# GpSimd leaves the chunk's tail and the S5 gate, the memory's norm takes other PSUM banks, and the final norm's factor is read from PSUM

## The chip, the cores and the metric

The kernel runs on one core of a Trainium2 chip. The metric is the device time of one execution, in microseconds (us): the median of several runs. A profiled execution of the same program gives the trace from which all durations below are taken. The engines are TensorE (PE, matmuls and transposes by matmul), VectorE (DVE), ScalarE (ACT), GpSimd (POOL) and SyncE (SP), which here issues all the DMAs.

## The reference

One decoder layer in float32 with 1024 tokens and width 1024. Its parts, cut to what matters here:

```python
def _mixer(xn, ...):
    proj = xn @ w_in                          # q, k, v, z, a, b and the S5 input u
    qkv = silu(_causal_dwconv(proj[..., OFF_Q:OFF_Z], conv_w))     # width 4, per channel
    g = -exp(dn_a_log) * softplus(a + dn_dt_bias); beta = sigmoid(b)
    o = _gated_delta_rule(l2norm(q) * dk**-0.5, l2norm(k), v, g, beta)
    o = o * rsqrt(mean(o * o, -1) + EPS)
    o = o * dn_norm_g * silu(z)               # 4 heads of 128
    y = gelu(_s5(u, ...))
    y = y * sigmoid(y @ s5_w_glu + s5_b_glu)  # the S5 gate, width 512
    return concatenate([o, y], -1) @ w_out

h = h + _mixer(_rmsnorm(h), ...)
h = h + _cross_attn(_rmsnorm(h), mem, ...)    # 256 memory tokens, themselves normalised:
                                              # mn = _rmsnorm(mem, norm_mem_g)
h = h + (silu(hn @ w_gate) * (hn @ w_up)) @ w_down
return _rmsnorm(h, norm_final_g)              # the final norm
```

## The kernel before, in words

Features lie on partitions (128 at a time) and tokens along the free dimension, in halves of 512. Each float32 operand of a large matmul is split into a high part (ACT, line 62) and the rest (line 63, on DVE or POOL), and each product is three matmuls (lines 79 to 81).

The kernel is written with a tile framework. Every tile comes from a pool with a fixed number of buffers; a tile that finds none free waits until an older one of its name has been read for the last time. The order of the instructions on each engine's queue is not the order of the text: the framework simulates a timeline at build time (`schedule_with_timeline_sim=True`), places each instruction where it becomes ready there, and takes the earlier one in the text where two are ready. The queues then run strictly in that order. `issue_after` and `keep_in_program_order` fix the order in a few places, none of which the diff touches.

PSUM has eight banks of 128 x 512 float32. The pool `pm` (name "mm") has three for the large products throughout. `p5` (name "aux") has one until the mixer ends. `px`, `pda`, `pdb`, `p6`, `ps`, `po` and, for the second half of the kernel, `pa` (five banks, name "aux") share the rest in turn.

The stages in the order of the text, with the functions that the change and the prediction's steps name:

1. `x_prep`, `in_tile` for the four S5 inputs, `s5_setup` and `s5_pre` (parameters of the S5 model; the product of line 334 uses p5), `zab` (z, a, b; z goes to DRAM as zD).
2. `gates` computes g and beta on small tiles (L545 writes g). Two products with a triangular matrix follow: L552 (copied by L554, its exponential by L556) and L558, whose copy `gr` (L560) goes to DRAM as gD. Each head later reads a row of gD back, spread over all partitions, as `d_Qg`.
3. `mem_prep` loads the memory, squares it, sums the squares over features (`rstd`, L120 to L129), spreads the factor over the partitions by four matmuls into a bank `rb` (L821), and multiplies the memory by it and by the gain (L826, eight instructions on DVE). The results are split on ACT and POOL and stay until `mem_proj` uses them.
4. For each of four heads: `in_tile` for k, q and v. A half tile is 24 matmuls into a bank of pm; L480 multiplies it by the norm's factor into `pre`; L489 (ACT) and three L491 (DVE) build the convolution in a bank of p5; L492 (ACT, silu) writes `it`. `dn_a` transposes k (L595), takes d_Qg through POOL (L583) and ACT (L584 to L586), copies two columns on DVE (L588, L589) and prepares the head's matrices; `dn_b` inverts them.
5. Eight chunks of 128 tokens. `dn_seq` carries the state of all four heads from chunk to chunk (L752, L754, L760, L761 on ACT, L766, L769) and leaves the chunk's output in a bank `po`. `dn_tail` normalises it, multiplies it by silu(z) and transposes it: squares on ACT (L791), L792, ten small rsqrt steps on DVE (L85 to L89), the product with the factor (L795, DVE), the product with z (L796, POOL), four transposes (L799), a split (L65, L66). Beside it run the memory's projections (`mem_proj`) and the S5 blocks (`s5_in`, `s5_out`).
6. `glu`, the S5 gate: for two halves and four row tiles, twelve matmuls into a bank of p5 or p6, a sigmoid on ACT (L909) into an SBUF tile, y from its two parts on DVE (L910), the product on POOL (L911), a split.
7. `out_acts`, `out_pair` (out projection), `mem_load` (whose tiles `kst` take buffers that the chunk stage frees), cross attention, then the feed-forward stage as Strassen products.
8. The last rows: for three pieces of 512, 256 and 256 tokens, `ff_down` and the residual add (L1368), squares and their sum, and `final`: the norm's factor spread by matmuls (`row_sums`, L143), copied to SBUF by ACT (`rowbc`, L139), then for eight row tiles a multiply on DVE (even ones, with the gain, L1380) or POOL (odd ones, L1378; their gain was applied before), and a store for every two.

Of the kernel before, what the change touches and what calls it, by code (L numbers as in the profile page):

```python
# [9 lines left out]
F32 = mybir.dt.float32  # L10
F32R = mybir.dt.float32r
I32 = mybir.dt.int32
AF = mybir.ActivationFunctionType
ALU = mybir.AluOpType
# [4 lines left out]
P = 128  # L19
NT = 1024  # L20
HT = 512
# [24 lines left out]
class Kernel:  # L46
# [478 lines left out]
    def gates(self, ab, cv):  # L525

        v, A = self.v, self.a
        ts, st, tt = v.tensor_scalar, v.scalar_tensor_tensor, v.tensor_tensor
        T = lambda n: cv.tile([P, 8, 4], F32, name=n, bufs=1)
        x, e, u, l, d, m = (T("gt_" + n) for n in "xeuldm")  # L530
        tt(out=x, in0=ab[:, :, 0:4], in1=self.dtb.unsqueeze(1).to_broadcast([P, 8, 4]), op=ALU.add)

        st(out=l, in0=x, scalar=-1.0, in1=x, op0=ALU.mult, op1=ALU.min)
        self.exact_exp(e, l, u, d, m)
        ts(out=u, in0=e, scalar1=1.0, scalar2=2.0, op0=ALU.mult, op1=ALU.add)
        v.reciprocal(out=u, in_=u)
        tt(out=u, in0=u, in1=e, op=ALU.mult)
        tt(out=d, in0=u, in1=u, op=ALU.mult)
        ts(out=l, in0=d, scalar1=2.0 / 17, scalar2=0.0, op0=ALU.mult, op1=ALU.add)
        for k in range(15, 1, -2):  # L540
            st(out=l, in0=l, scalar=2.0 / k, in1=d, op0=ALU.add, op1=ALU.mult)
        st(out=l, in0=l, scalar=2.0, in1=u, op0=ALU.add, op1=ALU.mult)
        st(out=l, in0=x, scalar=0.0, in1=l, op0=ALU.max, op1=ALU.add)
        g_ = T("gt_g")
        tt(out=g_, in0=l, in1=self.nega.unsqueeze(1).to_broadcast([P, 8, 4]), op=ALU.mult)  # L545
        beta = self.cp.tile([P, 8, 4], F32, name="beta")
        ts(out=x, in0=ab[:, :, 4:8], scalar1=-1.0, scalar2=0.0, op0=ALU.mult, op1=ALU.add)
        self.exact_exp(e, x, u, d, m)
        ts(out=e, in0=e, scalar1=1.0, scalar2=1.0, op0=ALU.add, op1=ALU.mult)
        v.reciprocal(out=beta, in_=e)  # L550
        ps = self.p5.tile([P, HT], F32, name="aux")
        self.te.matmul(ps[:, 0:32], self.UT, g_.rearrange("p a b -> p (a b)"), start=True, stop=True)  # L552
        gc = self.cp.tile([P, 8, 4], F32, name="gc")
        v.tensor_copy(out=gc, in_=ps[:, 0:32].rearrange("p (a b) -> p a b", a=8))  # L554
        eg = self.cp.tile([P, 8, 4], F32, name="eg")
        A.activation(out=eg, in_=gc, func=AF.Exp)  # L556
        ps = self.p5.tile([P, HT], F32, name="aux")
        self.te.matmul(ps[0:32, 0:P], g_.rearrange("p a b -> p (a b)"), self.UT, start=True, stop=True)  # L558
        gr = cv.tile([32, P], F32, name="gr", bufs=1)
        v.tensor_copy(out=gr, in_=ps[0:32, 0:P])  # L560
        self.load(self.gD, gr)
        self.gate = (beta, gc, eg)
        self.dnv = [self.cp.tile([P, 8, 4], F32, name="dn_" + n) for n in ("al", "b3n", "eq")]
# [216 lines left out]
    def dn_tail(self, c, po, dq, xs):  # L780

        v, A, g, te = self.v, self.a, self.g, self.te
        sh = [P, 4, P]
        eq = self.dnv[2][:, c, :]
        T = lambda name: self.slot(name).rearrange("p (h v) -> p h v", h=4)
        sz = T("sz")
        self.load(sz, self.zD[c].rearrange("p (h v) -> p h v", h=4))
        on = T("on")
        sso, ro, w4 = (dq.tile([P, 4], F32, name="d_" + n) for n in ("sso", "ro", "w4b"))
        for i in range(4):  # L790
            A.activation(out=on[:, i], in_=po[:, i], func=AF.Square, accum_out=sso[:, i:i + 1])  # L791
        v.scalar_tensor_tensor(out=sso, in0=sso, scalar=1.0 / P, in1=eq, op0=ALU.mult, op1=ALU.add)  # L792
        self.rsqrt(ro, sso, w4)
        on = T("on")
        v.tensor_tensor(out=on, in0=po, in1=ro.unsqueeze(2).to_broadcast(sh), op=ALU.mult)  # L795
        g.tensor_tensor(out=on, in0=on, in1=sz, op=ALU.mult)  # L796
        ps = self.po.tile(sh, F32, name="po")
        for i in range(4):
            te.transpose(ps[:, i], on[:, i], self.ident)  # L799
        o = slice((c % 4) * P, (c % 4 + 1) * P)  # L800
        self.split(ps, *(x[:, 0:4, o] for x in xs[c // 4]), self.dng)


    def mem_prep(self, cv):

        T = lambda n, i: self.tmp.tile([P, HT], F32, name=n, bufs=i)
        two = lambda t: t.rearrange("p (k t) -> p k t", k=2)
        raws = [T(n, 2) for n in ("res", "res", "fsg")] + [cv.tile([P, 4 + HT], F32, name="pre", bufs=3)[:, 4:]]
        acc = T("acc0", 1)
        for i, r in enumerate(raws):  # L810
            self.load(two(r), self.I["memT"][:, 2 * i:2 * i + 2])
            sq = T("sq", 2) if i else acc
            self.a.activation(out=sq, in_=r, func=AF.Square)
            if i:
                self.g.tensor_tensor(out=acc, in0=acc, in1=sq, op=ALU.add)
        self.g.tensor_tensor(out=acc[:, 0:NMEM], in0=acc[:, 0:NMEM], in1=acc[:, NMEM:], op=ALU.add)
        ps = lambda: self.p5.tile([P, HT], F32, name="aux")
        rs = self.rstd(acc, 2, "rsm", ps())
        rb = ps()
        for t in range(2):  # L820
            self.te.matmul(rb[:, t * P:(t + 1) * P], rs[:, t:t + 1].to_broadcast([P, P]), self.ident, start=True, stop=True)  # L821
        mh, ml = [], []
        for i, ns in enumerate((("fsg", "sq"), ("sq", "acc1"), ("acc0", "res"), ("res", "fsg"))):
            for j in range(2):
                r = two(raws[i])[:, j]
                self.v.scalar_tensor_tensor(out=r, in0=r, scalar=self.gain(2, 2 * i + j), in1=rb[:, 0:NMEM], op0=ALU.mult, op1=ALU.mult)  # L826
            h, l = (T(n, 1 if n[0] == "a" else 2).bitcast(F32R) for n in ns)
            self.split(raws[i], h, l, None, self.g)
            mh += [two(h)[:, j] for j in range(2)]
            ml += [two(l)[:, j] for j in range(2)]  # L830
        return mh, ml
# [58 lines left out]
    def glu(self, q8, xs):  # L890
        T = lambda n, k=2: q8.tile([P, HT], F32, name=n, bufs=k)
        ws = []
        for m in range(4):
            raw = q8.tile([P, 4, P], F32, name="yr", bufs=2)
            self.load(raw, self.I["w_glu"][m])
            wh, wl = (q8.tile([P, 4, P], F32R, name=n, bufs=4) for n in ("gwh", "gwl"))
            self.split(raw, wh, wl, None, self.g)
            ws.append((wh, wl))
        y8 = [[x[:, 4:8] for x in xs[h]] for h in range(2)]
        for h in range(2):  # L900
            yh, yl = y8[h]
            out = []
            for m in range(4):
                wh, wl = ws[m]
                ps = (self.p5, self.p6)[m % 2].tile([P, HT], F32, name="aux")
                for k in range(4):
                    self.mm3(ps, wh[:, k], wl[:, k], yh[:, k], yl[:, k], k == 0, k == 3)
                sg, yy = T("yr"), T("yy", 8)
                self.a.activation(out=sg, in_=ps, func=AF.Sigmoid, bias=self.bglu[:, m:m + 1])  # L909
                self.v.tensor_tensor(out=yy, in0=yh[:, m].bitcast(F32), in1=yl[:, m].bitcast(F32), op=ALU.add)  # L910
                self.g.tensor_tensor(out=yy, in0=yy, in1=sg, op=ALU.mult)  # L911
                out.append(yy)
            for m in range(4):
                self.split(out[m], yh[:, m], yl[:, m])
# [455 lines left out]
    def final(self, o, rs):  # L1370

        n = o.stop - o.start
        rb = self.tmp.tile([P, HT], F32, name="res", bufs=2)[:, 0:n]
        self.rowbc(rs, n // P, rb)
        for m in range(KD):
            dst = self.out_rows(m, o)
            if m % 2 == 1:
                self.g.tensor_tensor(out=dst, in0=dst, in1=rb, op=ALU.mult)  # L1378
            else:
                self.v.scalar_tensor_tensor(out=dst, in0=dst, scalar=self.gain(4, m), in1=rb, op0=ALU.mult, op1=ALU.mult)  # L1380
            if m % 2:
                h = o.start // HT
                src = self.hT[:, m // 2, 2 * h:2 * h + 2, o.start - h * HT:o.stop - h * HT]
                self.load(self.out[m - 1:m + 1].rearrange("m p t -> p m t")[:, :, o], src)
# [295 lines left out]
```

## Time and profile before

| | |
|---|---|
| median of 3 runs | 1603.62 us (1600.15 to 1607.66) |
| the profiled execution | 1605.2 us |
| its span in the trace | 1603.2 us |
| instructions | 20926 |
| mean granted clock of TensorE | 0.958 |

The trace's views used below are: the page (busy time and share of each engine, the chain that ended last), busy time by stretches, the waits (who waited for whom: total, times, longest), groups of instructions (either busy time and mean, or the shortest, median and longest duration), and the timeline (start, duration, engine, line, operation, output and inputs, how many, and in brackets how long the engine had been idle before and what ended that). All times are in us from the span's start, unless marked ns. A line number is that of the kernel before. L85 to L89 and other helpers serve several places; the tile's name tells which. In the names, `d_R` and `d_L` are also reused as spare buffers in the chunk stage: there L795 and L796 write `on` into d_R and read z from d_L. An "aux" tile may be in p5, p6 or pa.

### The profile page before, as it was taken

The page shows a single profiled execution, that of the slowest core. Times are in us where ns is not written, and L with a number is a line of the kernel's source. Part 1 is how long each engine was busy: PE and PEld are TensorE (multiplying, and loading weights), DVE is VectorE, ACT ScalarE, POOL GpSimd, SP SyncE. Part 2 cuts the span into 40 slices and gives each one's busy share as a digit, 9 for nine tenths or more (in the row PEclk, how much of TensorE's full clock was granted, in tenths as well). Part 3 has the DMA queues.
Part 4 walks back from the last instruction along what each step waited for, and adds up shares of the span by engine and source line. Part 5 has one row for each costly group of instructions (what it writes and reads, how often), then busy time and mean ns, then how long its engine had stood idle before and what let it go on. Part 6 is the DMA issues. An engine that isn't in the chain of part 4 may idle for free.

```text
span 1603.2 us, 20926 instructions
## 1 busy us (share of the span) xinstructions
PE 1457.7 (91%) x7326; PEld 1218.8 (76%) x7326; DVE 1188.9 (74%) x2164; ACT 634.7 (40%) x1137; POOL 655.9 (41%) x475
## 2 busy tenths in 40 slices
PE   6887699996978788999999999999999998999985
PEld 4787488886877576878888788888888886777864
DVE  8969489886699797775546697666666668899886
ACT  5222353452544563454443442333333334533322
POOL 6175234324552416620010443333333347766544
PEclk9999899997989988999999999999999999999997
DMA  7256454548688152245524414444444357444302
GB/s 224 80 164 199 134 133 124 140 119 293 213 291 265 47 197 105 79 131 171 171 92 165 144 33 145 149 142 139 145 137 137 112 168 251 149 146 150 126 10 105
DMA packets 146616, 237.49 MB, mean 148 GB/s; under 512 B 12464, under 2 KB 79440, under 8 KB 143952
## 3 DMA queue, kind: packets, MB, share of 16 engines
q1 hardware_dynamic: 146512, 236.17, 45.7%
q8 instruction: 57, 0.93, 0.2%
q14 instruction: 47, 0.39, 0.1%
HBM read 169.69 MB, written 68.53 MB: 149 GB/s over the span
## 4 chain that ended last, share of the span: by engine, by line
PE 53%; DVE 24%; DMA 9%; issue 5%; ACT 4%; POOL 3%; SPq 1%; DVEq 0%; POOLq 0%; ACTq 0%
PE aux L81 9%; PE aux L79 9%; PE aux L80 9%; PE mm L81 8%; PE mm L79 8%; PE mm L80 8%; DVE aux L491 2%; DVE wlo L63 1%; DVE d_R L675 1%; DMA s_wb<-in_s5bT 1%; DVE s_S L398 1%; POOL wlo L63 1%; DVE hT L1380 1%; DMA d_R<-LD 1%; DMA wraw<-in_w_xk 1%
## 5 line engine op out<-in xcount | busy, mean ns | idle before, releaser
L62 ACT ACTIVATE whi<-wraw 128x1024 fp32r<-128x1024 f32 (+2 forms) x152 | 139.7, 922 | 202.3 <-PE mm L80 67.3
L79 PE MATMUL mm<-AH,whi 128*128 128x512 f32 x448 | 178.4, 399 | 1.4 <-DVE hT L1325 1.4
L81 PE MATMUL mm<-AH,wlo 128*128 128x512 f32 x432 | 170.9, 396 | 0.0
L80 PE MATMUL mm<-AL,whi 128*128 128x512 f32 x408 | 161.3, 396 | 0.0
L150 POOL TENSOR_TENSOR acc<-acc,sq 128x512 f32<-128x512 f32 (+1 forms) x41 | 53.1, 1295 | 212.9 <-ACT sq L149 212.1
L63 DVE TENSOR_TENSOR wlo<-wraw,whi 128x1024 fp32r<-128x1024 f32 (+1 forms) x76 | 97.9, 1290 | 33.2 <-ACT whi L62 33.1
L1204 POOL TENSOR_TENSOR sg<-sg,ca 128x512 f32<-128x512 f32 x40 | 58.2, 1456 | 144.1 <-DVE sg L1197 92.7
L63 POOL TENSOR_TENSOR wlo<-wraw,whi 128x1024 fp32r<-128x1024 f32 x28 | 67.8, 2422 | 115.8 <-ACT whi L62 98.8
L79 PEld LDWEIGHTS mm<-AH,whi 128*128 128x128 f32 x448 | 84.6, 189 | 20.9 <-DVE hT L1325 2.9
L81 PEld LDWEIGHTS mm<-AH,wlo 128*128 128x128 f32 x432 | 81.5, 189 | 18.3 <-issue 0.4
L80 PEld LDWEIGHTS mm<-AL,whi 128*128 128x128 f32 x408 | 77.1, 189 | 16.6
L80 PE MATMUL aux<-AL,whi 128*128 128x512 f32 x216 | 85.0, 393 | 0.7 <-POOL AL L63 0.7
L79 PE MATMUL aux<-AH,whi 128*128 128x512 f32 x176 | 69.7, 396 | 0.0
L62 ACT ACTIVATE wlo<-graw 128x512 fp32r<-128x512 f32 x62 | 38.8, 626 | 62.7 <-PE aux L81 53.1
L81 PE MATMUL aux<-AH,wlo 128*128 128x512 f32 x160 | 63.4, 396 | 0.0
L491 DVE SCALAR_TENSOR_TENSOR aux<-pre,convw,aux 128x512 f32<-128x512 f32 x72 | 54.1, 751 | 8.3 <-ACT aux L489 7.5
L1202 ACT ACTIVATE ca<-ca 128x512 f32<-128x512 f32 x40 | 25.3, 633 | 83.5 <-DVE ca L1197 83.0
L63 POOL TENSOR_TENSOR wlo<-wb,whi 128x768 fp32r<-128x768 f32 x19 | 39.8, 2094 | 42.3 <-ACT whi L62 42.3
L81 PE MATMUL aux<-AH,whi 128*128 128x512 f32 x136 | 53.4, 392 | 0.0
L80 PEld LDWEIGHTS aux<-AL,whi 128*128 128x128 f32 x216 | 40.6, 188 | 10.6 <-POOL AL L63 1.4
L63 DVE TENSOR_TENSOR wlo<-graw,wlo 128x512 fp32r<-128x512 f32 x40 | 46.0, 1150 | 2.2 <-ACT wlo L62 2.2
L79 PE MATMUL aux<-AH,wlo 128*128 128x512 f32 x120 | 47.3, 394 | 0.0
(713 smaller groups left out, 4678.2 us busy)
## 6 DMA issues: line engine op xcount, KB each, us to landing
graw<-in_w_up SPq DMA_DIRECT2D x22, 512.0 KB
acc<-in_w_down SPq DMA_DIRECT2D x42, 256.0 KB
actD<-sg SPq DMA_DIRECT2D x40, 256.0 KB
WD<-acc SPq DMA_DIRECT2D x40, 256.0 KB
wraw<-in_w_in SPq DMA_DIRECT2D x16, 512.0 KB
d_X<-XD SPq DMA_DIRECT2D x8, 1024.0 KB
wraw<-AD SPq DMA_DIRECT2D x16, 512.0 KB
wraw<-VD SPq DMA_DIRECT2D x16, 512.0 KB
```

The source lines that it names most:

```text
L62: self.a.activation(out=hi, in_=src, func=AF.Copy)
L63: return (eng or self.v).tensor_tensor(out=lo, in0=src, in1=hi.bitcast(F32), op=ALU.subtract)
L79: mm(ps, wh, xh, start=first, stop=False)
L80: mm(ps, wh, xl, start=False, stop=False)
L81: mm(ps, wl, xh, start=False, stop=last)
L150: eng.tensor_tensor(out=acc, in0=acc, in1=tmp, op=ALU.add)
L398: v.tensor_tensor_scan(out=Zs[:, k, q], data0=self.m8[:, 2 * b + q:2 * b + q + 1].to_broadcast([P, P]), data1=Z[:, k, q], initial=0.0, op0 ...
L491: v.scalar_tensor_tensor(out=acc, in0=pre[:, 1 + i:1 + i + HT], scalar=cw(i), in1=acc, op0=ALU.mult, op1=ALU.add)
L675: tt(out=R[:, i, :, 0:i], in0=R[:, i, :, 0:i], in1=X[:, :, 0:i], op=ALU.mult)
L1202: A.activation(out=r, in_=r, func=AF.Silu)
L1204: g.tensor_tensor(out=r, in0=r, in1=sg[o], op=ALU.mult)
L1380: self.v.scalar_tensor_tensor(out=dst, in0=dst, scalar=self.gain(4, m), in1=rb, op0=ALU.mult, op1=ALU.mult)
```

## The change

- `gates` and `mem_prep`: the tiles for the gates' two products, for the memory's sum of squares and for its spread factor come from pm instead of p5.
- `dn_tail`: DVE multiplies the chunk's output by z instead of by the rsqrt factor; then ACT multiplies each of the four heads by its factor, as a per-partition scale. POOL's product is gone.
- `glu`: the sigmoid is written back into its own PSUM bank, and DVE multiplies from there. POOL's product and the SBUF tile for the sigmoid are gone.
- `final`: the DVE multiplies read the factor from its PSUM bank, and row tile 7 moves from POOL to DVE. POOL still reads ACT's copy in SBUF.

```diff
--- before.py
+++ after.py
@@ -548,13 +548,13 @@
         self.exact_exp(e, x, u, d, m)
         ts(out=e, in0=e, scalar1=1.0, scalar2=1.0, op0=ALU.add, op1=ALU.mult)
         v.reciprocal(out=beta, in_=e)
-        ps = self.p5.tile([P, HT], F32, name="aux")
+        ps = self.pm.tile([P, HT], F32, name="mm")
         self.te.matmul(ps[:, 0:32], self.UT, g_.rearrange("p a b -> p (a b)"), start=True, stop=True)
         gc = self.cp.tile([P, 8, 4], F32, name="gc")
         v.tensor_copy(out=gc, in_=ps[:, 0:32].rearrange("p (a b) -> p a b", a=8))
         eg = self.cp.tile([P, 8, 4], F32, name="eg")
         A.activation(out=eg, in_=gc, func=AF.Exp)
-        ps = self.p5.tile([P, HT], F32, name="aux")
+        ps = self.pm.tile([P, HT], F32, name="mm")
         self.te.matmul(ps[0:32, 0:P], g_.rearrange("p a b -> p (a b)"), self.UT, start=True, stop=True)
         gr = cv.tile([32, P], F32, name="gr", bufs=1)
         v.tensor_copy(out=gr, in_=ps[0:32, 0:P])
@@ -792,8 +792,9 @@
         v.scalar_tensor_tensor(out=sso, in0=sso, scalar=1.0 / P, in1=eq, op0=ALU.mult, op1=ALU.add)
         self.rsqrt(ro, sso, w4)
         on = T("on")
-        v.tensor_tensor(out=on, in0=po, in1=ro.unsqueeze(2).to_broadcast(sh), op=ALU.mult)
-        g.tensor_tensor(out=on, in0=on, in1=sz, op=ALU.mult)
+        v.tensor_tensor(out=on, in0=po, in1=sz, op=ALU.mult)
+        for i in range(4):
+            A.activation(out=on[:, i], in_=on[:, i], func=AF.Copy, scale=ro[:, i:i + 1])
         ps = self.po.tile(sh, F32, name="po")
         for i in range(4):
             te.transpose(ps[:, i], on[:, i], self.ident)
@@ -814,7 +815,7 @@
             if i:
                 self.g.tensor_tensor(out=acc, in0=acc, in1=sq, op=ALU.add)
         self.g.tensor_tensor(out=acc[:, 0:NMEM], in0=acc[:, 0:NMEM], in1=acc[:, NMEM:], op=ALU.add)
-        ps = lambda: self.p5.tile([P, HT], F32, name="aux")
+        ps = lambda: self.pm.tile([P, HT], F32, name="mm")
         rs = self.rstd(acc, 2, "rsm", ps())
         rb = ps()
         for t in range(2):
@@ -905,10 +906,10 @@
                 ps = (self.p5, self.p6)[m % 2].tile([P, HT], F32, name="aux")
                 for k in range(4):
                     self.mm3(ps, wh[:, k], wl[:, k], yh[:, k], yl[:, k], k == 0, k == 3)
-                sg, yy = T("yr"), T("yy", 8)
-                self.a.activation(out=sg, in_=ps, func=AF.Sigmoid, bias=self.bglu[:, m:m + 1])
+                yy = T("yy", 8)
+                self.a.activation(out=ps, in_=ps, func=AF.Sigmoid, bias=self.bglu[:, m:m + 1])
                 self.v.tensor_tensor(out=yy, in0=yh[:, m].bitcast(F32), in1=yl[:, m].bitcast(F32), op=ALU.add)
-                self.g.tensor_tensor(out=yy, in0=yy, in1=sg, op=ALU.mult)
+                self.v.tensor_tensor(out=yy, in0=yy, in1=ps, op=ALU.mult)
                 out.append(yy)
             for m in range(4):
                 self.split(out[m], yh[:, m], yl[:, m])
@@ -1370,14 +1371,18 @@
     def final(self, o, rs):
 
         n = o.stop - o.start
+        ps = self.pa.tile([P, HT], F32, name="aux")
+        self.row_sums(rs, n // P, ps)
         rb = self.tmp.tile([P, HT], F32, name="res", bufs=2)[:, 0:n]
-        self.rowbc(rs, n // P, rb)
+        self.a.activation(out=rb, in_=ps[:, 0:n], func=AF.Copy)
         for m in range(KD):
             dst = self.out_rows(m, o)
-            if m % 2 == 1:
+            if m in (1, 3, 5):
                 self.g.tensor_tensor(out=dst, in0=dst, in1=rb, op=ALU.mult)
+            elif m == 7:
+                self.v.tensor_tensor(out=dst, in0=dst, in1=ps[:, 0:n], op=ALU.mult)
             else:
-                self.v.scalar_tensor_tensor(out=dst, in0=dst, scalar=self.gain(4, m), in1=rb, op0=ALU.mult, op1=ALU.mult)
+                self.v.scalar_tensor_tensor(out=dst, in0=dst, scalar=self.gain(4, m), in1=ps[:, 0:n], op0=ALU.mult, op1=ALU.mult)
             if m % 2:
                 h = o.start // HT
                 src = self.hT[:, m // 2, 2 * h:2 * h + 2, o.start - h * HT:o.stop - h * HT]
```

## The prediction

> **What bounds the kernel now.** I read the page first, then busy time by stretches, then the waits and the timeline of the stretches where TensorE (PE) is not full.
>
> ```profile
> PE 1457.7 (91%) x7326; PEld 1218.8 (76%) x7326; DVE 1188.9 (74%) x2164; ACT 634.7 (40%) x1137; POOL 655.9 (41%) x475
> 700.00:1300.00 600.00, 596.74 (x2638) 486.55 (x2639) 380.93 (x595) 221.38 (x384) 159.11 (x112) 1.00 0.40 133
> 168.50:188.80 20.30, 12.82 (x60) 10.28 (x58) 1.79 (x12) 3.17 (x4) 6.31 (x3) 0.91 0.62 182
> 181.30:196.00 14.70, 0.04 (x2) 0.03 (x1) 7.11 (x16) 8.09 (x11) 9.21 (x6) 0.63 0.21 65
> 196.00:270.00 74.00, 72.29 (x368) 60.67 (x368) 64.45 (x150) 31.49 (x68) 27.57 (x13) 0.98 0.44 122
> 440.00:506.00 66.00, 53.34 (x403) 51.88 (x404) 59.48 (x144) 29.54 (x73) 27.74 (x27) 0.90 0.81 269
> 506.00:545.00 39.00, 35.11 (x217) 30.17 (x216) 31.78 (x76) 22.83 (x54) 17.85 (x13) 1.00 0.45 147
> 545.00:556.00 11.00, 4.58 (x21) 3.27 (x19) 6.68 (x16) 4.83 (x15) 4.58 (x3) 0.90 0.00 0
> 1560.00:1603.20 43.20, 23.06 (x136) 22.04 (x136) 24.72 (x57) 11.13 (x28) 20.58 (x23) 0.71 0.28 97
> ```
>
> Behind each stretch stand its length, then the busy time (and instructions) of PE, weight loads, VectorE (DVE), ScalarE (ACT) and GpSimd (POOL), then PE's granted clock. From 700 to 1300 PE is full, and the change touches nothing there. It touches three places where PE is not full: a hole at 181 to 196, the chunk stage from 440 to 556, where DVE is the fullest engine, and the end. So the sum is made from these three.
>
> **The hole: the gates and the memory's norm.** The waits there, and the timeline around it:
>
> ```profile
> PE da L595 <- ACT it L492: 14.7, 1, 14.7
> 150.92 0.19 DVE L545 TENSOR_TENSOR gt_g<-gt_l,nega 128x32 f32<-128x32 f32 x1
> 160.43 0.30 PE L552 MATMUL aux<-gt_g,cst 128*128 128x32 f32 x2
> 160.50 0.67 DVE L480 TENSOR_TENSOR pre<-mm,rbx 128x512 f32<-128x512 f32 x1
> 168.22 0.27 DVE L560 COPY gr<-aux 32x128 f32<-32x128 f32 x1
> 168.65 0.23 PE mm L79
> 175.14 0.62 SPq L54 DMA_DIRECT2D gD<-gr  x1
> 186.62 2.36 POOL L63 TENSOR_TENSOR wlo<-wraw,whi 128x1024 fp32r<-128x1024 f32 x1
> 188.79 0.22 DVE L588 COPY dn_al<-d_Qg 128x8 f32<-128x8 f32 x1 [13.67 <-ACT d_Qg L586]
> 191.27 0.86 DVE L826 SCALAR_TENSOR_TENSOR pre<-pre,gains,aux 128x256 f32<-128x256 f32 x2
> 192.23 0.69 ACT L489 ACTIVATE aux<-pre,convw 128x512 f32<-128x512 f32 x1 [0.21 <-DVE pre L826]
> 192.97 2.32 DVE L491 SCALAR_TENSOR_TENSOR aux<-pre,convw,aux 128x512 f32<-128x512 f32 x3
> ```
>
> The first convolution's input is ready at 161.2 (L480), yet its first step, L489, starts at 192.23, right behind the last L826. L826 applies the memory's norm. The norm's factor lies in the single p5 bank, which the convolution's accumulator needs too. L826 in turn stands on DVE behind L588, which waits for the gate's round trip through DRAM (gr, gD, d_Qg). So PE's transposes (L595) of the finished tile come 14.7 us late.
>
> After: the factor lies in pm, p5 is free at 161, and no convolution needs L826. From 168.5 to 188.8 DVE was busy 1.8 of 20.3 us. The work that now may go there is five convolutions (5 x 2.3), three L480 (3 x 0.7) and L826 (188.9 to 192.1, 3.2): 16.8 us, and it fits. What is late next is a weight: its low part (POOL, 186.62) stands behind the same round trip and ends at 189.0, and PE would reach it at 181.3 + 24 x 0.23 + 0.6 for the transposes = 187.4, so 1.6 us of wait come back.
>
> The norm's factor now holds one of pm's three banks until L826 is done; a bank is a half tile, 24 x 0.23 = 5.5 us of PE. The gates' two products (L552, L558) go from p5 to pm as well: g was ready at 151.1 and its product ran at 160.4, when p5 came free. With it the copy gr and the DMAs gD and d_Qg move forward on SP's queue, past the loads that held gD from 168.5 to 175.1; that shortens L588's wait and takes from nothing but those loads. If the order stays, it brings nothing.
>
> Bounds: 14.7, plus 1.1 for the slow matmuls that follow a hole (clock 0.63), is the most; nothing if L491 stays behind L588; a loss of 5.5 if only pm's bank counts. PE is full from 196 to 270 (72.29 of 74), so what it wins there it keeps. 14.7 + 1.1 - 1.6 = 14.2, less 2.2 (my estimate, two thirds of L826) for norm steps that still come first on DVE: **12 us gained** (-5.5 to 16).
>
> **The chunk's tail and the S5 gate.** Timeline, groups of lines (busy, mean ns) and waits:
>
> ```profile
> L87 DVE TENSOR_TENSOR d_w4b<-d_ro 128x4 f32<-128x4 f32 x24 | 9.0, 374 | 0.6
> L89 DVE SCALAR_TENSOR_TENSOR d_ro<-d_w4b,d_ro 128x4 f32<-128x4 f32 x24 | 6.4, 268 | 0.6
> L88 DVE SCALAR_TENSOR_TENSOR d_w4b<-d_w4b,d_sso 128x4 f32<-128x4 f32 x24 | 6.0, 248 | 0.6
> 546.48 0.16 DVE L792 SCALAR_TENSOR_TENSOR d_sso<-d_sso,dn_eq 128x4 f32<-128x4 f32 x1 [5.66 <-ACT d_R L791]
> 547.10 1.30 POOL L911 TENSOR_TENSOR yy<-yy,yr 128x512 f32<-128x512 f32 x1 [3.53 <-ACT yr L909]
> 547.28 1.14 DVE L89 SCALAR_TENSOR_TENSOR d_ro<-d_w4b,d_ro 128x4 f32<-128x4 f32 x1
> 552.97 1.59 POOL L796 TENSOR_TENSOR d_R<-d_R,d_L 128x512 f32<-128x512 f32 x1 [1.95 <-issue]
> 554.62 1.11 PE L799 MATMUL po<-cst,d_R 128*128 128x128 f32 x4 [6.15 <-POOL d_R L796]
> 555.86 1.74 SPq L54 DMA_DIRECT2D kst<-memD  x4
> L791 ACT ACTIVATE d_R<-po x32: 269/278/300, 439.6 to 546.1; 128x128 f32<-128x128 f32 x32
> POOL d_R L796 <- issue: 11.2, 3, 7.6
> POOL d_R L796 <- DVE d_R L795: 8.3, 4, 2.4
> ```
>
> A DVE step of 0.16 us takes 1.14 beside a POOL multiply; both read two operands from SBUF. The 72 rsqrt steps took 9.0 + 6.4 + 6.0 = 21.4 instead of 72 x 0.16 = 11.5, so 9.9 us were lost beside POOL work of every kind. The 16 multiplies that go are 37% of POOL's 43 instructions here, so 3.7 of these.
>
> The last chunk's tail is on the path: the next stage's loads (kst, 555.86) need its buffers, 9.4 us after L792. After the change: L792 and ten rsqrt steps at 0.2 from start to start (546.48 to 547.28 is four), 2.2; two gate products and two splits on DVE between them at 0.68, 2.7; four scaled copies on ACT at 0.28, 1.1; one ACT step between, 0.7; the last transpose, 0.5. That is 7.2: 2.2 gained. Of the 3.7, 2.0 lie in that tail, and of the other 1.7 I count half, 0.8, since waits cover the rest. The tail's product stays on DVE, with another operand.
>
> Edits at no cost, and their cover: six of the eight new gate products on DVE (8 x 0.68 = 5.4) lie under PE's gate matmuls, the last two are counted above; 28 of the 32 scaled copies (8 x 1.1 = 8.8) lie in ACT's idle time, 36 of 66 us. With the cover gone they cost 14.2. Waits that are added: p5 and p6 come free after the DVE product and not after the sigmoid, 0.7 us later, while the next tile's 12 matmuls (2.8) run in the other bank; the z tile is now waited for on DVE, the rsqrt steps behind it, but two slots let its load go out two chunks ahead. The most is 9.4 - 3.8 (rsqrt, copies and transpose alone) + 1.7 = 7.3. **3 us gained** (-14 to 7).
>
> **The final norm.** Timeline, two lines' durations, and one piece of the chain:
>
> ```profile
> 1572.08 6.92 DVE L1380 SCALAR_TENSOR_TENSOR hT<-hT,gains,res 128x512 f32<-128x512 f32 x4 [1.88 <-ACT res L139]
> 1572.12 6.33 POOL L1378 TENSOR_TENSOR hT<-hT,res 128x512 f32<-128x512 f32 x4 [2.33 <-PE aux L81]
> 1579.47 0.66 PE L120 MATMUL aux<-ones,acc 128*128 128x64 f32 x2 [4.47 <-DVE hT L1368]
> 1588.90 3.64 DVE L1380 SCALAR_TENSOR_TENSOR hT<-hT,gains,res 128x256 f32<-128x256 f32 x4 [1.22 <-ACT res L139]
> 1596.35 3.31 POOL L1378 TENSOR_TENSOR hT<-hT,res 128x256 f32<-128x256 f32 x4 [4.09 <-ACT res L139]
> L1325 DVE TENSOR_TENSOR Q<-Q,aux x48: 672/675/689, 1384.5 to 1545.6; 128x512 f32<-128x512 f32 x48
> 207.18 1.23 DVE d_kd L600
> ```
>
> Four 512-wide DVE steps take 6.92 here beside POOL's four. With one operand in PSUM a DVE step stays at 0.672 to 0.689 (L1325, 48 times, POOL busy beside many). So five steps make 3.4 in the first piece: 3.5 gained, and PE waited 4.47 for their end. In the second, five of half the width at 0.36 make 1.8: 1.8 gained. The third ends on POOL, whose three steps without a two-operand DVE step beside them I put at 0.73 each, an estimate from L911's 1.30 for twice the width plus a little: 2.2 for 3.3, 1.1 gained. The bank is now held until the last DVE step, which keeps PE from one 256-wide tile, 0.7. The stores follow their pairs. 3.5 + 1.8 + 1.1 - 0.7 = 5.7: **6 us gained** (2 to 8).
>
> I do not count the time of ACT's copy: L600 started at 207.18, when ACT was done with the same bank, though it needs no result of ACT, so DVE will wait for the copy as before. The Trainium skill, "PSUM — Partial Sum Buffer", section "PSUM bank collisions raise a hardware error", has the same: two engines' accesses to one bank are put in order, reads too. Against the change speaks the Trainium skill, "VectorE: DVE Perf Modes", section "The TRN2 errata": a VectorE step has 120 fixed cycles from PSUM and 58 from SBUF. By that, an estimate of 0.065 us more for each of 23 steps, the gain would be 1.5 us less; the trace does not agree, L1325 reads PSUM at 0.675.
>
> **Sum.** The profiled execution took 1605.2 with its span of 1603.2, 1.6 above the median of 1603.62. 1605.2 - 12 - 3 - 6 = 1584.2; I say 1584. The runs of one kernel lie up to 0.5% (8 us) apart, which is the bound of "same" below.
>
> **The rivals.** First, the hole stays. The order of each queue comes from a timeline that the framework simulates at build time, and it may still put L588 ahead of the convolutions; it did put it ahead of L826. Against it: L480 was ready 27 us before L588. Then 1605.2 - 3 - 6 = 1596.2.
>
> Second, slower: ACT inherits POOL's wait. POOL waited 19.5 us (11.2 + 8.3) before L796, at no one's cost. If the scaled copies stand on ACT ahead of the state chain's own copy (L761) while rsqrt is late on a crowded DVE, every chunk waits. 19.5 + 8.8 = 28.3 lost in place of the 3 gained: 1605.2 - 12 - 6 + 28.3 = 1615.5. It decides from 18 us, 2.6 in each of seven chunks. Against it: with fewer POOL multiplies rsqrt is less late.
>
> Third, the new order makes waits of its own in places that the change doesn't name and eats about half: 1595 (1588 to 1602).
>
> **How the numbers follow.** All three gains, 0.54, its own range 1574 (16 + 7 + 8) to 1592 (8 + 1 + 4). The hole stays, 0.20, and the new order, 0.15, each about half below 1595.6, which is 8 under the median. Slower, 0.11. Faster 0.54 + 0.10 + 0.07 = 0.71, same 0.18, slower 0.11. The range from 1573 to 1601 leaves out the slower case and the far end of the third.
>
> **What would show it.** L489's first start near 161 to 170, and no idle time over 5 us before the first L595; no POOL rows at L796 or in the gate; about 7 us from the last L792 to the kst loads; the final norm's DVE steps at 0.68 and 0.42. I am wrong if L588 still stands before the convolutions, if ACT idles before the scaled copies with L761 behind them, or if PE waits for a pm bank between 100 and 190.

## The result, and the profile after

The changed kernel takes 1590.44 us (median of 4 runs, 1587.80 to 1592.99) against 1605.64 of the kernel before (4 runs, three of them those of the table above). These medians lie 15.2 us apart; the ratio on record is 0.9872, 95% interval 0.9840 to 0.9904, which is some 20 us. Measured again beside 17 runs of the kernel before it was 0.9874 (0.9857 to 0.9891; 1589.6 against 1610.37), and there medians and ratio agree on 20 us. So it is 15 to 21 us faster, and 20 by the measurement with more runs. The prediction said 1584 and faster; the time is 6 us above it and inside the range. The parts did not bring what it gave them, as the experiments show.

The profiled execution took 1592.23 us, its span 1590.2. First the busy time by stretches. Columns: length, then busy time (and instructions) of PE, weight loads, DVE, ACT and POOL, then PE's granted clock. Before:

```profile
0.00:160.00 160.00, 126.63 (x713) 106.41 (x714) 132.54 (x386) 54.15 (x84) 83.51 (x95) 0.91 0.53 166
160.00:200.00 40.00, 24.79 (x109) 19.78 (x108) 18.07 (x45) 11.89 (x16) 11.61 (x7) 0.83 0.46 137
200.00:260.00 60.00, 60.00 (x305) 50.34 (x304) 50.80 (x122) 29.22 (x65) 20.86 (x10) 1.00 0.51 142
0.00:560.00 560.00, 466.15 (x2903) 408.69 (x2903) 444.07 (x1105) 231.58 (x457) 243.25 (x208) 0.93 0.56 173
540.00:560.00 20.00, 9.73 (x50) 7.79 (x48) 11.01 (x24) 6.60 (x17) 5.86 (x4) 0.85 0.12 42
600.00:625.00 25.00, 16.13 (x64) 13.18 (x65) 16.18 (x24) 6.99 (x12) 14.87 (x6) 0.80 0.27 98
```

After, with the page's line of busy times:

```profile
PE 1465.5 (92%) x7326; PEld 1222.4 (77%) x7326; DVE 1189.4 (75%) x2175; ACT 644.4 (41%) x1171; POOL 626.7 (39%) x456
...
0.00:160.00 160.00, 122.34 (x682) 103.11 (x682) 129.37 (x374) 54.13 (x84) 83.08 (x95) 0.89 0.52 161
160.00:200.00 40.00, 36.77 (x165) 30.51 (x166) 29.10 (x69) 18.60 (x37) 14.96 (x8) 0.90 0.61 183
200.00:260.00 60.00, 55.38 (x279) 46.01 (x278) 48.21 (x122) 24.80 (x43) 21.82 (x11) 0.97 0.43 126
0.00:560.00 560.00, 473.01 (x2903) 414.30 (x2903) 443.20 (x1110) 242.62 (x492) 220.53 (x192) 0.92 0.56 174
540.00:560.00 20.00, 17.59 (x88) 14.41 (x86) 13.42 (x31) 12.31 (x30) 0.00 (x0) 1.00 0.21 73
600.00:625.00 25.00, 24.43 (x98) 19.45 (x99) 23.48 (x35) 11.64 (x20) 10.76 (x7) 0.93 0.32 112
1560.00:1590.20 30.20, 17.86 (x107) 16.71 (x106) 17.00 (x56) 8.77 (x21) 13.12 (x16) 0.67 0.39 139
```

What the reader is to see is PE's idle time, length less busy. The hole at 160 to 200 goes from 15.2 to 3.2 us, as predicted, but PE now idles 4.3 more before 160 and 4.6 more from 200 to 260, and up to 540 the sums are equal: 83.6 and 84.6 (93.9 - 10.3 and 87.0 - 2.4). The idle time that went lies at 540 to 560 (10.3 to 2.4), at 600 to 625 (8.9 to 0.6) and behind 1560 (20.1, by the prediction's row for 1560 to 1603.2, to 12.3). These three make 24.0 against a change of 20.8 in the whole span (145.5 to 124.7). The third the prediction had; the second it did not name; the first it had put down to the chunk tail alone. But the first is no gain in time. At 540 the changed kernel is 39 matmuls behind (2816 done, before 2855) and catches up by 560, where both traces have 2903 done, as many of each shape: in time it has won nothing by then. The 6.9 us of idle time that it saved went into as much more busy time for as many matmuls (473.0, before 466.2; PE's granted clock is 0.92, before 0.93), and the profiled gain of 13 us lies behind.

The waits of PE. Columns: total, times, longest. Before:

```profile
PE aux L370 <- DMA wraw<-in_w_xk: 8.1, 1, 8.1
PE aux L81 <- POOL wlo L63: 9.5, 1, 9.5
```

After:

```profile
PE mm L822 <- DVE rsm L89: 5.0, 1, 5.0
PE aux L370 <- DMA s_U<-uD: 12.1, 1, 12.1
```

The 5.0 us are new: the spread of the memory norm's factor (L822) now stands in PE's queue right behind its column sums, and PE waits there for DVE's rsqrt. The 12.1 us come where the S5 stage's first loads are late. PE waited there before too (8.1). It now comes 4.6 us later (375.7, before 371.1), but the loads leave SP's queue later still, by 8.4 us. Before and after:

```profile
367.12 0.87 SPq L54 DMA_DIRECT2D s_W<-SD  x1
375.54 3.19 SPq L54 DMA_DIRECT2D s_W<-SD  x1
```

### The profile page after: what moved, and what is told of

Its sections match the earlier page's. It is cut to its first block, busy times and chain, and to the rows that moved or that the text cites. A ratio compares the mean times of both kernels' runs of the same rounds, so it can differ in the third digit from the quotient of the medians.

```text
span 1590.2 us, 20950 instructions
## 1 busy us (share of the span) xinstructions
PE 1465.5 (92%) x7326; PEld 1222.4 (77%) x7326; DVE 1189.4 (75%) x2175; ACT 644.4 (41%) x1171; POOL 626.7 (39%) x456
## 4 chain that ended last, share of the span: by engine, by line
PE 61%; DVE 21%; DMA 8%; issue 3%; ACT 3%; POOL 2%; SPq 1%; POOLq 0%; DVEq 0%; ACTq 0%
PE mm L79 9%; PE mm L81 9%; PE aux L81 9%; PE aux L79 9%; PE mm L80 9%; PE aux L80 9%; PE db L689 1%; DVE wlo L63 1%; DMA s_wb<-in_s5bT 1%; DVE aux L491 1%; DVE AL L66 1%; DMA d_R<-LD 1%; SPq L54 1%; ACT whi L62 1%; DVE d_R L675 1%
## 5 line engine op out<-in xcount | busy, mean ns | idle before, releaser
L81 PE MATMUL mm<-AH,wlo 128*128 128x512 f32 x432 | 171.9, 398 | 0.0
L81 PEld LDWEIGHTS mm<-AH,wlo 128*128 128x128 f32 x432 | 81.9, 190 | 18.5
L81 PE MATMUL aux<-AH,wlo 128*128 128x512 f32 x160 | 63.5, 397 | 0.0
L491 DVE SCALAR_TENSOR_TENSOR aux<-pre,convw,aux 128x512 f32<-128x512 f32 x72 | 54.0, 750 | 10.3 <-ACT aux L489 8.9
L81 PE MATMUL aux<-AH,whi 128*128 128x512 f32 x136 | 53.6, 394 | 0.0
```

The source lines that it names most:

```text
L81: mm(ps, wl, xh, start=False, stop=last)
L491: v.scalar_tensor_tensor(out=acc, in0=pre[:, 1 + i:1 + i + HT], scalar=cw(i), in1=acc, op0=ALU.mult, op1=ALU.add)
```

## The experiments

Every ratio is against the kernel before on the same chip. Its medians were 1610.37, 1610.37 and 1610.96 us in the three groups.

**The banks alone.** In `gates` and `mem_prep`:

```
-        ps = self.p5.tile([P, HT], F32, name="aux")
+        ps = self.pm.tile([P, HT], F32, name="mm")
...
-        ps = lambda: self.p5.tile([P, HT], F32, name="aux")
+        ps = lambda: self.pm.tile([P, HT], F32, name="mm")
```

> The kernel before, with only the PSUM banks of the gates (L551, L557) and of the memory's norm (L818) moved from p5 to pm; chunk tail, S5 gate and final norm as before. Theory 1 (the hole's gain is earned at 196 and given back before 400): the first L489 starts at 161 to 175 instead of 192, the last in_proj work of the stage ends some 10 us earlier, but the stage's end at about 560 is where it was; the whole is 1600 to 1605 us, ratio 0.997 to 1.0. Rival (the hole's gain carries to the end, as the prediction counted it): 1605 - 12 = 1593, ratio 0.992. What tells them apart is PE's idle time summed up to 560: 94 us as before, or 82.

Measured: 0.9951 (0.9933 to 0.9969), 1602.6 us. Stretches of its trace:

```profile
160.00:200.00 40.00, 36.05 (x152) 29.32 (x153) 27.12 (x64) 18.78 (x37) 13.66 (x8) 0.88 0.54 166
380.00:400.00 20.00, 7.45 (x42) 7.24 (x42) 13.62 (x41) 5.53 (x11) 6.11 (x6) 0.66 0.96 321
540.00:560.00 20.00, 17.36 (x87) 13.96 (x86) 15.80 (x29) 10.29 (x24) 12.34 (x8) 1.00 0.23 67
600.00:625.00 25.00, 21.33 (x85) 16.45 (x84) 24.02 (x36) 9.92 (x18) 6.61 (x5) 0.93 0.36 126
0.00:560.00 560.00, 477.21 (x2886) 416.18 (x2886) 450.73 (x1095) 229.51 (x451) 239.14 (x205) 0.90 0.56 172
```

8 us, between the two theories. By the sign that was to tell them apart the rival would be right: PE's idle time up to 560 is 82.8 us, before 93.9. But the sign misleads, for only 2886 matmuls are done by then (before 2903), at a granted clock of 0.90 (before 0.93): less idle time is not more work done. The hole is closed (idle 4.0), 12.6 us of idle time stand at 380 to 400, and the gains at 540 and at 600 are there although tail and gate are as before.

**The tail and the S5 gate alone.**

```
-        v.tensor_tensor(out=on, in0=po, in1=ro.unsqueeze(2).to_broadcast(sh), op=ALU.mult)
-        g.tensor_tensor(out=on, in0=on, in1=sz, op=ALU.mult)
+        v.tensor_tensor(out=on, in0=po, in1=sz, op=ALU.mult)
+        for i in range(4):
+            A.activation(out=on[:, i], in_=on[:, i], func=AF.Copy, scale=ro[:, i:i + 1])
...
-                self.g.tensor_tensor(out=yy, in0=yy, in1=sg, op=ALU.mult)
+                self.v.tensor_tensor(out=yy, in0=yy, in1=ps, op=ALU.mult)
```

> The kernel before, with only the chunk's tail and the S5 gate changed (no GpSimd multiply in either; ACT scales by the norm's factor, DVE multiplies by the gate); banks and final norm as before. Theory 1 (the prediction's 3 us, plus what the new order does to the stage behind it): GpSimd's single weight split in the output projection, which took 11.8 us at 597 beside an unbroken run of DVE steps, may or may not be caught again; 1601 to 1604 us if it is, 1593 to 1597 if not. Rival (ACT inherits the wait): 1610 or more, with PE waiting for ACT at L800. What tells them apart: PE's idle time from 440 to 560, and the longest GpSimd split between 585 and 625.

Measured: 1.0012 (0.9996 to 1.0028), 1611.0 us: nothing, or a little lost. A wait of PE, and a row of ACT's timeline:

```profile
PE po L800 <- ACT d_R L797: 5.5, 2, 4.2
...
458.76 1.28 ACT L797 ACTIVATE d_R<-d_R,d_ro 128x128 f32<-128x128 f32 x4 [3.98 <-DVE d_ro L89]
```

PE's wait for POOL's product (L799, 6.15 before) is now one for ACT's copies. At 458.76 the slower rival's mechanism is seen: ACT stands 3.98 us for rsqrt, with the state chain's L761 right behind the copies. It is one chunk, not every one.

**The final norm alone.** Everything up to it keeps its order.

```
-        self.rowbc(rs, n // P, rb)
+        self.row_sums(rs, n // P, ps)
+        self.a.activation(out=rb, in_=ps[:, 0:n], func=AF.Copy)
...
-            if m % 2 == 1:
+            if m in (1, 3, 5):
                 self.g.tensor_tensor(out=dst, in0=dst, in1=rb, op=ALU.mult)
+            elif m == 7:
+                self.v.tensor_tensor(out=dst, in0=dst, in1=ps[:, 0:n], op=ALU.mult)
...
-                self.v.scalar_tensor_tensor(out=dst, in0=dst, scalar=self.gain(4, m), in1=rb, op0=ALU.mult, op1=ALU.mult)
+                self.v.scalar_tensor_tensor(out=dst, in0=dst, scalar=self.gain(4, m), in1=ps[:, 0:n], op0=ALU.mult, op1=ALU.mult)
```

> The kernel before, with only the final norm changed: the factor read from PSUM by DVE, row tile 7 on DVE, GpSimd with three tiles of each piece. Only the end differs, so this is the one part that can't reorder anything before it. Theory 1 (DVE's steps are no longer stretched beside GpSimd): DVE's first piece 2.7 us instead of 6.9, the time 1605 - 7.8 = 1597, ratio 0.995. Rival (the last 7.8 us of the gain came from an earlier arrival and not from this edit): 1602 to 1605, ratio 0.998 to 1.0.

Measured: 0.9965 (0.9950 to 0.9981), 1603.5 us: 5.6 us. The ends of the interval touch both theories (0.995 and 0.998); the trace decides for the first: DVE's four steps of the first piece take 2.72 us, not 6.92, so the gain is this edit's and not an earlier arrival's.

**The operand alone.** DVE reads the factor from PSUM; POOL keeps its four row tiles.

> The kernel before, in whose final norm only DVE's four steps of each piece read the factor from PSUM; GpSimd keeps its four row tiles of each piece, from SBUF. Theory 1 (a DVE step with one operand in PSUM is not held up by GpSimd): four DVE steps in 2.7 us in the first piece where they took 6.9, with GpSimd busy beside them at 1.3 to 1.6 a step. Rival (it was GpSimd's fourth tile): DVE's steps still take over 1 us each, 4.5 us or more for four.

Its timeline (the line numbers are its own), one run of 1605.81 us:

```profile
1580.30 2.72 DVE L1382 SCALAR_TENSOR_TENSOR hT<-hT,gains,aux 128x512 f32<-128x512 f32 x4 [1.88 <-ACT res L1376]
1580.34 5.04 POOL L1380 TENSOR_TENSOR hT<-hT,res 128x512 f32<-128x512 f32 x4 [2.34 <-PE aux L81]
```

Before, the same eight steps took 6.92 and 6.33. The operand alone brings DVE to 0.68 a step and POOL to 1.26, so it is the operand and not the moved tile. The moved tile then shortens POOL's part.

**The first output pair's weight splits on DVE.** The kernel before; only this line of `out_pair` differs:

```
-            self.split(src[n], w[:, 0:4], w[:, 4:8], None, (self.v, self.g)[x % 2])
+            self.split(src[n], w[:, 0:4], w[:, 4:8], None, self.v if mp == 0 else (self.v, self.g)[x % 2])
```

> The kernel before, unchanged but for three weight splits of the first pair of the output projection (in out_pair, mp = 0), which go from GpSimd to DVE; the changed parts of this case are all left as they were. Theory 1 (the 7 to 8 us that the changed kernel wins at 600 to 620, which no step of the prediction named, is GpSimd's split held up by DVE: 11.83 us where 1.3 are usual): with that split on DVE PE's wait of 9.5 us at 597 goes, three DVE steps of 0.68 come in its place, and the time is 1605 - 7.5 = 1597.5, ratio 0.995. Rival (PE would have waited there for DVE's own queue anyhow, or gets the wait one step later): 1603 to 1606, ratio 0.999 to 1.0.

Measured: 0.9965 (0.9951 to 0.9978), 1604.8 us, and PE's wait at L81 is gone. 5.6 us came (3.5 to 7.9 by the interval), where 7.5 were said: theory 1 holds. What that wait was, in the timeline of the kernel before (the first DVE row is the step that runs when POOL starts; the last is the 17th of the steps that follow it without a break):

```profile
596.99 11.82 POOL L63 TENSOR_TENSOR wlo<-fsg,wlo 128x512 fp32r<-128x512 f32 x1 [4.30 <-ACT wlo L62]
596.77 0.68 DVE L952 TENSOR_TENSOR res<-res,AH 128x512 f32<-128x512 f32 x1
...
607.01 0.68 DVE L955 TENSOR_TENSOR res<-AH,res 128x512 f32<-128x512 f32 x1
```

And the same split after the change:

```profile
593.38 1.61 POOL L63 TENSOR_TENSOR wlo<-fsg,wlo 128x512 fp32r<-128x512 f32 x1 [2.56 <-ACT wlo L62]
593.15 0.69 DVE L63 TENSOR_TENSOR AL<-res,AH 128x512 fp32r<-128x512 f32 x1
593.75 1.77 DVE L983 TENSOR_TENSOR wraw<-wraw 128x512 f32<-128x512 f32 x1
```

POOL's split takes 11.82 us while DVE runs step after step with two SBUF operands, one start every 0.60 us, and none of them is stretched. After the change one DVE step is stretched to 1.77 and POOL is done in 1.61. In both traces POOL starts 0.22 to 0.23 us into a DVE step, so its start alone does not decide which of the two waits; what does is not shown. The split was held up in the runs of the tail alone, the final norm alone and the operand alone (PE waits of 10.2, 9.4 and 9.5), and passed in all the runs with a moved bank that left it on POOL, but for one, told below.

**The banks, with those splits on DVE.**

> The kernel before with two edits: the banks moved (as in the run of the banks alone), and the three weight splits of the first output pair on DVE (as in the run of that alone). Banks alone gave 0.9951, the splits alone 0.9965. Theory 1 (the banks' gain in the time is mostly that their new order lets GpSimd's split through at 600, and the hole's gain at 196 is given back by 540): 0.994 to 0.997, no more than the better one of the two alone. Rival (the hole is worth its own share, the splits theirs): 0.9951 x 0.9965 = 0.9916.

Measured: 0.9959 (0.9943 to 0.9975), beside 0.9951 and 0.9965 for either alone; the rival's 0.9916 lies outside the interval. So, as far as the time shows, the two gains are mostly the same one: the banks' 8 us are mostly the passed split.

**Banks and final norm, without tail and gate; and the whole change again.**

> The changed kernel without its chunk tail and S5 gate (both as before). The parts alone gave 0.9951 (banks), 1.0012 (tail and gate) and 0.9965 (final norm), whose product is 0.9928, while the whole change gave 0.9872. Theory 1 (the tail and the gate are worth something only where the banks have moved: they take GpSimd out of DVE's way, and without the banks the held-up weight split at 600 eats it): this run 0.9951 x 0.9965 = 0.9916, so 1597 us against 1610 of before, and the whole stays 7 us ahead of it. Rival (the parts add up, tail and gate are worth nothing): 0.991 to 0.993, the same as the whole change measured beside it.

> The changed kernel, unaltered, beside the other three. Theory 1 (the parts help each other): 0.987 as at first, some 20 us less than before. Rival (the parts add): 0.991 to 0.993, 12 to 14 us less.

Measured: 0.9889 (0.9869 to 0.9909) and 0.9874 (0.9857 to 0.9891). Tail and gate are worth 0.0015 on top of the rest, which the intervals do not tell from nothing. The theory that they help once the banks have moved falls. Nor do the parts quite multiply: banks and final norm gave 0.9889 where the product is 0.9916 (0.9892 to 0.9940), the whole 0.9874 where it is 0.9928 (0.9899 to 0.9957); only in the second case do the two intervals not overlap. A piece of bookkeeping with the means of the timed runs shows where the rest may be: the mean time, multiplied by the mean granted clock, falls from 1538.1 to 1535.1 with the banks, to 1537.4 with tail and gate and to 1534.3 with the final norm, together 7.5 us, and with the whole change by 8.9 (1538.6 to 1529.7). In this product the parts add up to within 1.4 us. The other 12 us of the whole change go with a higher granted clock: 0.9553 to 0.9556 before, 0.9582, 0.9538 and 0.9565 for the parts, 0.9612 for banks and final norm, 0.9625 for all. That does not make the clock the cause. It falls behind waits of PE (last section), so a new order of the waits changes it too, and why it rises more with the parts together than apart stays open. By the same product the banks with the splits on DVE bring 5.2 us, where they bring 3.0 and 4.0 alone; so that those two gains are the same one holds for the time, and the product leaves it open.

**Either bank move alone.** The norm's (L818), then the gates' (L551, L557):

> The kernel before with only the memory norm's two banks moved from p5 to pm (L818); the gates' products stay in p5. The prediction held that this bank alone closes the hole and that the gates' banks bring nothing if the order stays. Theory 1 (the norm's bank does it): the first L595 at 186 to 190 instead of 196 without a wait for L492; PE's idle time from 160 to 200 is 2 to 5 us instead of 15. Rival (both moves are needed, since the gates' round trip through DRAM stays late on SP): L588 still stands late, and PE waits 8 us or more before the first L595.

> The kernel before with only the gates' two banks moved from p5 to pm (L551, L557); the norm's factor stays in p5, whose bank the first convolution needs. Theory 1 (the norm's bank holds up the convolution): the first L489 still comes right behind the last L826, wherever that lies; if the norm's steps come no earlier than before, PE still waits about 15 us before the first L595. Rival (it was the gates' place in the order that held the norm up): L826 moves forward by 10 us or more with the gates, the hole shrinks to under 6 us, and no wait of 5 us at the norm's spread comes in its place.

Measured: 0.9943 (0.9924 to 0.9963) and 0.9919 (0.9890 to 0.9949). PE's first stretch with the norm's bank alone:

```profile
160.00:200.00 40.00, 39.36 (x177) 32.20 (x178) 29.30 (x60) 18.87 (x38) 15.04 (x8) 0.94 0.60 184
```

With the gates' banks alone, and its timeline:

```profile
160.00:200.00 40.00, 40.00 (x183) 32.72 (x182) 25.97 (x69) 17.96 (x29) 13.53 (x9) 1.00 0.57 178
...
178.48 0.87 DVE L826 SCALAR_TENSOR_TENSOR pre<-pre,gains,aux 128x256 f32<-128x256 f32 x2
179.45 0.69 ACT L489 ACTIVATE aux<-pre,convw 128x512 f32<-128x512 f32 x1 [0.21 <-DVE pre L826]
```

Either move closes the hole by itself (idle 0.6 and 0.0; with the norm's bank the first L595 is at 185.9, without a wait). With the gates' banks alone the convolution still stands right behind the norm, as the theory of p5 has it, but the norm comes 12.8 us sooner, the rival's way. Neither run has a wait at the norm's spread, and PE waits 6.7 and 6.9 us at L370. With both moves (the banks alone) these waits are 4.4 and 12.1. So the waits that took the hole's gain back came with the two moves together. In time either move alone did at least as well as both (0.9951), but the intervals overlap, so that is not shown to be better.

**The norm's spread later in the queue.** The changed kernel with `mem_prep` cut in two at L821; the second half is written behind the first `in_tile` of the head loop.

> The changed kernel with one thing moved: the spread of the memory norm's factor (L822) and what follows it in mem_prep are written behind the first in_proj tile of the head loop, not ahead of it, so that TensorE's queue has some 50 matmul groups between the column sums (L120) and the spread. Theory 1 (the wait of 5.0 us at L822, which the change put there, costs what it shows, and DVE's 3 us of L827 stood ahead of the first convolution): PE's wait at 158 to 163 goes, the first L489 starts 3 to 8 us earlier than 173.8, and the time is 0 to 5 us less than that of the changed kernel, depending on how much is given back before 540. Rival (what is won before 250 is always given back at the first loads of S5, near 390): the same time as the changed kernel within 2 us, with PE's wait for s_U longer by what was won.

Measured: 0.9863 (0.9841 to 0.9885), 1587.1 us. The first L489 is at 169.0 and no wait at the spread is left. Two of PE's waits and a stretch:

```profile
PE aux L370 <- DMA s_W<-SD: 6.7, 1, 6.7
PE aux L81 <- POOL wlo L63: 9.1, 1, 9.1
...
0.00:560.00 560.00, 485.73 (x2997) 423.54 (x2998) 449.78 (x1124) 251.99 (x505) 219.94 (x192) 0.93 0.57 176
```

At 560 it has 94 matmuls more behind it than either kernel (2997 to 2903) and 74.3 us of idle time, not 87.0 as the changed kernel: the early gain is not always given back. The wait at S5's first loads is 6.7, and not longer than 12.1 as the rival has it, so the rival falls. By the time alone it would not: 2.5 us less than the changed kernel, with overlapping intervals. Then the split was held up, in this order too, and took 9.1 of it.

**The same, with the splits on DVE.**

> The changed kernel with two more edits: the memory norm's spread written behind the first in_proj tile (as in the run of that alone, 0.9863, in which GpSimd's split at 583 was held up again and PE waited 9.1 us for it), and the three weight splits of the first output pair on DVE. Theory 1 (whether that split is held up is decided by the order around it and is worth what the run of the splits alone showed, 0.0035): 0.9863 - 0.0035 = 0.983, 1583 us, which would be the fastest version of all. Rival (DVE's queue is the limit there and PE waits for it all the same): 0.986 to 0.988.

Measured: 0.9847 (0.9819 to 0.9874), 1586.1 us, the lowest ratio of all. Of the 0.0035 expected from the splits 0.0016 came; the interval holds the theory's 0.983 and most of the rival's range, so it does not decide. It also overlaps that of the changed kernel, so it is the best version measured but not shown to be better.

## Why the prediction was right or wrong

**The hole.** The mechanism was right. From the timeline after:

```profile
163.23 1.20 PE L822 MATMUL mm<-cst,rsm 128*128 128x128 f32 x4 [5.03 <-DVE rsm L89]
173.80 0.69 ACT L489 ACTIVATE aux<-pre,convw 128x512 f32<-128x512 f32 x1 [4.52 <-DVE pre L480]
188.03 1.03 PE L595 MATMUL da<-cst,it 128*128 128x128 f32 x8
```

L489 starts at 173.80 (said: 161 to 170; before 192.23), and PE reaches L595 without a wait. One sign, "no idle time over 5 us before the first L595", failed by the 5.03 at L822. The local gain, 12.0 us of idle time at 160 to 200, is of the predicted size. Two steps failed. First, "what it wins there it keeps", argued from a PE that was full from 196 to 270 in the old order. The new order put the spread into PE's queue with nothing between it and its column sums (5.0 us), made small waits at 200 to 260, and sent the S5 stage's first loads out 8.4 us later, so that PE waited 12.1 us for them, not 8.1. Why they go out later is not settled. This is the mechanism of the third rival, to which I gave 0.15. I had asked what would be late next on DVE and POOL, but not who stands behind the moved matmuls on PE's own in-order queue. Second, "if the order stays, it brings nothing" of the gates' banks: the order did not stay, and they close the hole alone. In time the banks brought 8 us, and with the split out of the way about 1 (0.9965 to 0.9959).

**Tail and gate.** The term failed: 3 gained was predicted, between 4.5 lost and 0.6 gained was measured. These groups of the rsqrt steps after (busy, mean ns), and the scaled copies (shortest/median/longest ns), show the terms that failed:

```profile
L89 DVE SCALAR_TENSOR_TENSOR d_ro<-d_w4b,d_ro 128x4 f32<-128x4 f32 x24 | 7.1, 294 | 0.5
L88 DVE SCALAR_TENSOR_TENSOR d_w4b<-d_w4b,d_sso 128x4 f32<-128x4 f32 x24 | 7.0, 292 | 0.4
L87 DVE TENSOR_TENSOR d_w4b<-d_ro 128x4 f32<-128x4 f32 x24 | 6.8, 284 | 0.4
...
L797 ACT ACTIVATE d_R<-d_R,d_ro x32: 384/387/407, 448.7 to 551.1; 128x128 f32<-128x128 f32 x32
```

The 72 steps take 20.9 us, not 21.4 - 3.7: beside the remaining POOL work nearly as many are stretched (10 over 0.2 us, before 11). The copies take 0.387, not 0.28; the row I took, L791, is a square from PSUM without a scale for each partition. The last tail, from L792 at 543.87 to the kst loads at 554.47, takes 10.6 us and not 7.2. Gate products and splits lie between its DVE steps, the last of which ends at 550.1 (6.3 us, said 4.9), and the transposes (553.84) stand behind gate matmuls on PE's queue, 2.3 us after the last copy. That does not cost what it would have before, as the new order leaves gate matmuls beside it. Before, the gate's products and the tail's transposes:

```profile
L911 POOL TENSOR_TENSOR yy<-yy,yr x8: 1284/1298/1689, 528.0 to 549.3; 128x512 f32<-128x512 f32 x8
L799 PE MATMUL po<-cst,d_R x32: 270/272/473, 455.4 to 555.3; 128*128 128x128 f32 x32
```

After:

```profile
L912 DVE TENSOR_TENSOR yy<-yy,aux x8: 675/683/690, 537.3 to 562.6; 128x512 f32<-128x512 f32 x8
L800 PE MATMUL po<-cst,d_R x32: 270/273/421, 449.2 to 554.2; 128*128 128x128 f32 x32
```

The gate ran out 6 us before the last transposes; now it outlasts them by 8. That, and not a shorter tail, is why PE idles less at 540 to 560. The banks alone have it too, with tail and gate as before: their last gate product starts at 566.8, their last transpose at 560.6.

**The final norm.** Right in mechanism and nearly in size: 6 predicted, 5.6 measured (3 to 8).

```profile
1566.52 2.72 DVE L1385 SCALAR_TENSOR_TENSOR hT<-hT,gains,aux 128x512 f32<-128x512 f32 x4 [2.80 <-ACT res L1377]
1578.07 1.66 DVE L1385 SCALAR_TENSOR_TENSOR hT<-hT,gains,aux 128x256 f32<-128x256 f32 x4 [1.22 <-ACT res L1377]
1583.94 2.10 POOL L1381 TENSOR_TENSOR hT<-hT,res 128x256 f32<-128x256 f32 x3 [3.73 <-ACT res L1377]
```

0.68 and 0.42 a step, POOL's three in 2.10 (said 2.2), DVE still behind ACT's copy. The rule on slower PSUM reads, weighed in the prediction, does not show: 0.68 from PSUM against 0.68 of the SBUF steps above.

**What was not named.** POOL's split at 597, 9.5 us of PE's time on the chain of the kernel before, was in the trace. A new order can lose it: that of the banks did, that of tail and gate did not. I had looked for PE's idle time where the edits are. The sum of 21 us came out near the measured 20 by luck: this gain, and what goes with a higher clock, stood in for two that failed.

## What to carry to other kernels

In a kernel whose queues are laid out by a planner, test a local edit against the whole order: list the largest single waits of the trace outside the edited stages too, since a new order can lose or make each of them, and here one of 9.5 us decided as much as the edit. When a wait of PE goes, look next at what stands behind the moved matmul on PE's own queue, and at whether the next stage's loads can come any sooner. Where DVE and GpSimd work side by side, give DVE's step one operand from PSUM: that was the one gain here that came as worked out.

## What the hardware showed that I had not expected

One GpSimd instruction can be held up by a whole run of DVE instructions, not by one: 11.82 us for 1.3 beside 17 DVE steps of two SBUF operands (rows above), none of which was delayed. The Trainium skill, "SBUF — State Buffer", section "Who interferes with whom", says that such a DVE step contends with a GpSimd read and that issue order decides who blocks. The trace agrees with the first: one of the two was stretched in either order. It does not bear out the second: POOL started 0.22 to 0.23 us into a DVE step in both traces, and waited for 17 further steps in one and for none in the other.

A wait of PE can cost more than its length. PE's clock after the change, behind a wait of 2.25 us (to 231.09) and behind the 12.1 us at L370 (to 387.75):

```profile
231.09:232.59 1.50, 1.50 (x11) 1.41 (x12) 1.32 (x8) 0.81 (x2) 0.00 (x0) 1.00 0.89 325
387.80:389.30 1.50, 1.50 (x7) 1.50 (x8) 1.33 (x6) 0.19 (x1) 0.00 (x0) 0.50 1.01 364
390.80:392.30 1.50, 1.50 (x9) 1.50 (x9) 1.28 (x3) 0.57 (x2) 0.83 (x1) 0.50 1.05 412
393.80:395.30 1.50, 1.50 (x14) 1.37 (x13) 1.50 (x7) 1.06 (x1) 0.00 (x0) 1.00 1.06 395
```

Behind the short wait it stays full. Ahead of the long one it is full too (1.00 from 374.0 to 375.6), and behind it half for some 5 us, so about 2.5 us of work are lost on top of the 12.1. I had counted such a loss once (1.1 for the hole) and not for the waits that took its place. The Trainium skill, "TensorE: Matmul & The Clock Gate", section "Part 1: The HAM clock gate", has half clock after at least one idle window of some 3.4 us, and full clock after at least one busy one. The trace agrees: half clock behind 12.1 us of waiting, and full again after some 5 us of work. A wait of 2.10 us (252.81 to 254.91) is followed by half clock as well (0.50 from 257.91 to 259.41), so a wait shorter than that window can be enough.
